# Small matrix products of two recurrent mixers, issued in pairs on the two halves of the TensorE array

## The chip, the cores and the metric

The kernel runs on one core of one Trainium2 chip. The metric is device time in microseconds; the kernel before takes 1673.71 us, the median of 3 runs (1672.53 to 1675.28). The engines of the core work side by side and in program order, each through its own list: TensorE (PE, matrix products; the loads of its stationary operand are listed apart as PEld), VectorE (DVE), ScalarE (ACT), GpSimd (POOL), and SyncE (SP), which here only issues DMA transfers.

## The reference

Two layers, each a mixer and a mixture of experts, over 256 frames of 1024 channels. The mixer sends one projection into three recurrent mixers over chunks of 64 frames: gated DeltaNet (4 heads, state 128x128), retention, and Mamba-2 SSD (2 groups of 8 heads, state 128 by 8x64). The two that matter here:

```python
# gated DeltaNet, per chunk (k, u, w, q of 64 rows; sol = triangular solve)
def step(state, inp):
    q_c, k_c, u_c, w_c, dec_c = inp
    delta = u_c - jnp.einsum('bhlk,bhkv->bhlv', w_c, state)
    state = dec_c[..., None, None] * state + jnp.einsum('bhlk,bhlv->bhkv', k_c, delta)
    return state, jnp.einsum('bhlk,bhkv->bhlv', q_c, state)

# SSD: inside a chunk
y = jnp.einsum('bghcij,bghcjp->bghcip', wmat, xh)
# SSD: from chunk to chunk
def step(state, inp):
    c_c, b_c, x_c, lc_c, dt_c = inp
    y_c = jnp.einsum('bgln,bghnp->bghlp', c_c, state) * jnp.exp(lc_c)[..., None]
    wr = jnp.exp(lc_c[..., -1:] - lc_c) * dt_c
    state = (jnp.exp(lc_c[..., -1])[..., None, None] * state
             + jnp.einsum('bgln,bghlp->bghnp', b_c, x_c * wr[..., None]))
    return state, y_c
```

DeltaNet reads a state that already holds the chunk; SSD reads the state before the chunk. The three outputs are projected, gated, summed and projected again; then a layer norm. The experts are top-2 of 8 in one of 4 groups, 32 experts in all, whose weights are read whole in every layer.

## The kernel before

Frames lie in two tiles of 128 (`tt`), so two chunks of 64 stand in one tile, the even one on partitions 0 to 63 and the odd one on 64 to 127 (`par`, `ps`). A layer has two stages. In the mixer stage, `main` walks 26 blocks of projections (`ORDER`), each cut into pieces of 24 or so matmuls; the weights are split into a high and a low part by ACT (L251) and DVE (L239) and multiplied in three products (`mm3`). Beside it `Weave` steps generators, one step a piece: `delta_chain` (A), `ret_chain` (B), `ssd_chain` (C) and what writes their outputs (`delta_out`, `ret_out`, `ssd_out`). The order on each engine is then set by a scheduler that places every instruction when its simulated operands are ready, so a product of a chain stands between projection products. In the expert stage, 1 MB weight tiles stream in through a ring of buffers (`W`, `ring`), and the buffers come free as PE uses them up.

TensorE multiplies a stationary operand of up to 128 rows by 128 columns. A product with 64 rows lies on the upper or the lower row half (its operands start at partition 0 or 64), one with 64 columns on one column half (its output starts at partition 0 or 64).

The tiles that matter. In `delta_chain`, per chunk c: `pks` = k of the chunk times the old state (L728, four heads, 64 columns), `vb` corrected by it on DVE (L732), `pd` and `dl` (the solve applied, L738 and ACT), `pS` (state increment) and `st` (the new state, DVE), `po` = q times the new state (L761, four heads, 64 columns). In `ssd_chain`, per tile tt and group g: `xdt`, `xw`, `xd` (scaled inputs), `crh`, `crl`, `pcr`, `crm` (decay matrix `dc`), then for both chunks `pi` = c times the old state (64 columns, 512 wide), `pcS` = b times `xw` (64 rows, 512 wide), `cst` the new state (DVE, POOL), `py` = `dc` times `xdt` (eight heads, 64x64); the sum of them is `y`, kept under the name `xdt`. `ssd_out` multiplies y by a gate (POOL, L968), takes squares (ACT) and a root (`crs`), scales (DVE, L981), and `out_T` transposes it (`poT`, L788). `px`, `pn`, `pT` are the 64x64 products of the DeltaNet solve (`bmm`), which walk heads in the outer loop and halves in the inner one.

Of the kernel before, what the change touches and what calls it, by code (L numbers as in the profile page):

```python
# [150 lines left out]
def trunk_kernel(ctx: ExitStack, tc: tile.TileContext, x_in, w_in, w_br, w_g, w_u, w_d, smalls, lnp, consts, out,  # L151
# [95 lines left out]
    def mm(o, l, r, start=True, stop=True):  # L247
        return PE.matmul(o, l, r, start=start, stop=stop)  # L248
# [100 lines left out]
    for l in range(layers):  # L349
# [240 lines left out]
        def delta_chain():  # L590
# [125 lines left out]
            st = None  # L716
# [2 lines left out]
            sso = M(8, "sso")  # L719
            for c in range(4):  # L720
                tt, par = c // 2, c % 2
                ps = slice(64 * par, 64 * par + 64)
                if c:

                    pk = P("pks")
                    for h in range(4):
                        a = (h % 2) * 256 + c * 64
                        mm(pk[ps, h * 128:(h + 1) * 128], kT[h // 2][:, a:a + 64], st[:, h * 128:(h + 1) * 128])  # L728
                    for h in range(4):
                        hs = slice(h * 128, (h + 1) * 128)  # L730
                        n = 4 * tt + h
                        DVE.scalar_tensor_tensor(vb[tt][ps, hs], pk[ps, hs], ckb[ps, n:n + 1], vb[tt][ps, hs],  # L732
                                                 op0=OP.mult, op1=OP.add)
                    yield
                pd = P("pd")
                for h in range(4):
                    hs = slice(h * 128, (h + 1) * 128)
                    mm(pd[ps, hs], Tt[ps, (4 * tt + h) * 64:(4 * tt + h) * 64 + 64], vb[tt][ps, hs])  # L738
                dl = T("dl", True)
                act(dl[ps], pd[ps])  # L740
                yield
                pS = P("pS")
                for h in range(4):
                    hs = slice(h * 128, (h + 1) * 128)
                    mm(pS[:, hs], kend[tt][ps, hs], dl[ps, hs])
                ns = T("st", True)
                if c == 0:
                    DVE.tensor_copy(ns, pS)
                else:
                    for h in range(4):  # L750
                        hs = slice(h * 128, (h + 1) * 128)
                        DVE.scalar_tensor_tensor(ns[:, hs], st[:, hs], ex[:, 2 + par, tt, h:h + 1], pS[:, hs],
                                                 op0=OP.mult, op1=OP.add)
                st = ns
                yield
                if par == 0:
                    po = P("po")
                for h in range(4):
                    hs = slice(h * 128, (h + 1) * 128)
                    a = (h % 2) * 256 + c * 64  # L760
                    mm(po[ps, hs], qT[h // 2][:, a:a + 64], st[:, hs])  # L761
                if par == 1:
                    o = T("ao")
                    DVE.tensor_copy(o, po)
                    junk = T("junk", True)
                    for h in range(4):
                        hs = slice(h * 128, (h + 1) * 128)
                        act(junk[:, hs], o[:, hs], AF.Square, accum_out=sso[:, 4 * tt + h:4 * tt + h + 1])
                    R["ao"].append(o)
# [113 lines left out]
        def ssd_chain():  # L883
# [23 lines left out]
            for tt in range(NT):  # L907
                for g in range(2):
                    hs = slice(4 + 8 * g, 12 + 8 * g)
                    p = P("pxt")  # L910
                    for q in range(4):
                        ch = 4 * g + q
                        PE.transpose(p[:, q * 128:(q + 1) * 128],
                                     xc[ch // 2][:, (ch % 2) * 256 + tt * 128:(ch % 2) * 256 + tt * 128 + 128], ident)
                    xdt, xw, xd = T("xdt"), T("xw", True), T("xd", True)
                    DVE.tensor_mul(o8(xdt), o8(p), bc(spl[:, tt, hs, None], 64))
                    DVE.tensor_mul(o8(xd), o8(p), bc(B["dsk"][:, 8 * g:8 * g + 8, None], 64))
                    POOL.tensor_mul(o8(xw), o8(xdt), bc(ex[:, 1, tt, hs, None], 64))
                    dp = T("crh", True, F32R), T("crl", True, F32R)
                    for d, g_ in zip(dp, R["gcp"]):  # L920
                        POOL.tensor_mul(o8(d), C["e64b"], bc(g_[:, tt, hs, None], 64))
                    yield
                    pr = P("pcr")
                    for d in dp:
                        mm(pr, R["bo_r"], d, d is dp[0], d is dp[1])
                    dc = T("crm", True)
                    yield
                    DVE.tensor_sub(o8(dc), bc(gc[:, tt, hs, None], 64), o8(pr))
                    act(dc, dc, AF.Abs)
                    act(dc, dc, AF.Exp, scale=-1.0)  # L930
                    POOL.tensor_mul(o8(dc), o8(dc),
                                    cb[:, None, (2 * tt + g) * 64:(2 * tt + g) * 64 + 64].to_broadcast([128, 8, 64]))
                    yield
                    yield
                    py, pi = P("py"), P("pi")
                    for par in range(2):
                        c = 2 * tt + par
                        ps = slice(64 * par, 64 * par + 64)
                        if c:
                            a = g * 256 + c * 64  # L940
                            mm(pi[ps], cT[:, a:a + 64], sts[g])
                        if c < 3:
                            pS = P("pcS")
                            mm(pS, btok[ps, (2 * tt + g) * 128:(2 * tt + g) * 128 + 128], xw[ps])
                            ns = T("cst", True)
                            if c == 0:
                                DVE.tensor_copy(ns, pS)
                            else:
                                POOL.tensor_mul(o8(ns), o8(sts[g]), bc(ex[:, 2 + par, tt, hs, None], 64))
                                DVE.tensor_add(ns, ns, pS)  # L950
                            sts[g] = ns
                        for n in range(8):
                            mm(py[ps, n * 64:n * 64 + 64], dc[ps, n * 64:n * 64 + 64], xdt[ps, n * 64:n * 64 + 64])
                        yield
                    y = xdt
                    rows = slice(64, 128) if tt == 0 else slice(0, 128)
                    DVE.tensor_add(y, xd, py)
                    DVE.tensor_mul(o8(xd[rows]), o8(pi[rows]), bc(ex[rows, 0, tt, hs, None], 64))
                    POOL.tensor_add(y[rows], y[rows], xd[rows])
                    R["cy"][tt, g] = y  # L960
                    yield
# [513 lines left out]
```

## Time and profile before

| | |
|---|---|
| runs | 1672.53, 1673.71, 1675.28 us; median 1673.71 |
| profiled execution | 1675.43 us, span 1673.8 us, mean granted clock 0.951 |
| PE busy | 1402.3 us (84%) |
| DVE, ACT, POOL busy | 630.8, 507.9, 180.7 us |
| DMA | 518.93 MB, mean 310 GB/s |
| chain that ended last | PE 51%, DMA 46%, DVE 2% |

The span is what the trace covers from first to last instruction; the execution is 1.6 us longer. Busy is the time in which at least one instruction of an engine ran. Matmuls are pipelined: one that lasts 0.28 us may be followed by the next after 0.12, so starts say more than durations. A float32 product stands in the trace as two matmul records. The chain is followed back from the last instruction, at each step to what released it.

### The profile page before, as it was taken

The page shows a single profiled execution, that of the slowest core. Times are in us where ns is not written, and L with a number is a line of the kernel's source. Part 1 is how long each engine was busy: PE and PEld are TensorE (multiplying, and loading weights), DVE is VectorE, ACT ScalarE, POOL GpSimd, SP SyncE. Part 2 cuts the span into 40 slices and gives each one's busy share as a digit, 9 for nine tenths or more (in the row PEclk, how much of TensorE's full clock was granted, in tenths as well). Part 3 has the DMA queues.
Part 4 walks back from the last instruction along what each step waited for, and adds up shares of the span by engine and source line. Part 5 has one row for each costly group of instructions (what it writes and reads, how often), then busy time and mean ns, then how long its engine had stood idle before and what let it go on. Part 6 is the DMA issues. An engine that isn't in the chain of part 4 may idle for free.

```text
span 1673.8 us, 25789 instructions
## 1 busy us (share of the span) xinstructions
PE 1402.3 (84%) x10568; PEld 891.2 (53%) x10568; DVE 630.8 (38%) x1216; ACT 507.9 (30%) x983; POOL 180.7 (11%) x146
## 2 busy tenths in 40 slices
PE   8999999999967729766699999999998677287775
PEld 8999878995312203221199988789843122022211
DVE  7888667663000000000288876676620000000002
ACT  6856558541000000000067564585310000000000
POOL 0321233200000000000004111332000000000000
PEclk9999999999989869989889999999999999699888
DMA  9544333779999999999974342338799999999996
GB/s 379 193 129 150 102 101 126 282 294 387 421 422 420 420 422 421 421 422 421 393 293 152 127 152 77 126 112 324 285 387 420 421 422 420 421 421 421 422 420 253
DMA packets 90410, 518.93 MB, mean 310 GB/s; under 512 B 10032, under 2 KB 10416, under 8 KB 41904
## 3 DMA queue, kind: packets, MB, share of 16 engines
q1 hardware_dynamic: 90288, 517.24, 77.7%
q8 instruction: 85, 1.39, 0.3%
q14 instruction: 37, 0.30, 0.1%
HBM read 516.15 MB, written 1.05 MB: 309 GB/s over the span
## 4 chain that ended last, share of the span: by engine, by line
PE 51%; DMA 46%; DVE 2%; issue 0%; ACT 0%; SPq 0%; DVEq 0%
DMA w<-in_w_u_dram 16%; DMA w<-in_w_d_dram 15%; DMA w<-in_w_g_dram 14%; PE g L248 8%; PE pbr L248 6%; PE cx L248 3%; PE pout L248 3%; PE cz L248 3%; PE pg L248 2%; PE pdn L248 2%; PE cbc L248 1%; PE pu L248 1%; PE aq L248 1%; PE bq L248 1%; PE az L248 1%; PE av L248 1%
## 5 line engine op out<-in xcount | busy, mean ns | idle before, releaser
L239 DVE TENSOR_TENSOR hi<-w,hi 128x512 fp32r<-128x512 f32 x400 | 322.9, 822 | 106.0 <-ACT hi L251 41.0
L1278 DVE TENSOR_TENSOR hr<-h,pu 128x256 f32<-128x256 f32 x32 | 16.7, 598 | 743.2 <-PE pu L248 743.2
L251 ACT ACTIVATE hi<-w 128x512 fp32r<-128x512 f32 x400 | 244.3, 628 | 168.9 <-PE pbr L248 43.9
L248 PE MATMUL pg<-w,xg 128*32 128x512 f32 x1024 | 184.6, 646 | 112.9 <-DMA w<-in_w_g_dram 112.7
L248 PE MATMUL pu<-w,xg 128*32 128x512 f32 x1024 | 196.6, 688 | 73.4 <-DMA w<-in_w_u_dram 73.4
L248 PE MATMUL pdn<-w,ht 128*32 128x512 f32 x1024 | 146.6, 603 | 29.9 <-DMA w<-in_w_d_dram 17.4
L248 PEld LDWEIGHTS pg<-w,xg 128*32 128x32 f32 x1024 | 39.9, 117 | 244.8 <-issue 142.6
L248 PEld LDWEIGHTS pu<-w,xg 128*32 128x32 f32 x1024 | 44.1, 122 | 212.9 <-DMA w<-in_w_u_dram 131.2
L248 PE MATMUL g<-xh,hi 128*128 128x256 f32 x768 | 143.0, 285 | 0.0
L248 PEld LDWEIGHTS g<-xh,hi 128*128 128x128 f32 x768 | 120.6, 191 | 2.5 <-issue 2.2
L248 PE MATMUL g<-xl,hi 128*128 128x256 f32 x384 | 110.1, 287 | 0.0
L251 ACT ACTIVATE h<-pg 128x512 f32<-128x512 f32 x16 | 9.6, 597 | 320.3 <-PE pg L248 320.3
L248 PEld LDWEIGHTS pdn<-w,ht 128*32 128x32 f32 x1024 | 35.6, 110 | 126.8 <-issue 67.8
L248 PE MATMUL pbr<-yh,hi 128*128 128x256 f32 x512 | 95.2, 285 | 0.0
L251 ACT ACTIVATE xg<-pxg 128x512 f32<-128x512 f32 (+1 forms) x18 | 10.3, 573 | 276.3 <-PE pxg L248 276.3
L1233 POOL TENSOR_TENSOR oh<-oh,cmb 128x256 f32<-128x256 f32 x16 | 10.0, 622 | 775.4 <-DVE oh L1232 708.2
L251 ACT ACTIVATE os<-pdn 128x512 f32<-128x512 f32 x32 | 19.1, 597 | 228.6 <-PE pdn L248 228.6
L248 PEld LDWEIGHTS pbr<-yh,hi 128*128 128x128 f32 x512 | 80.6, 192 | 2.4 <-issue 2.3
L248 PE MATMUL pxg<-oh,x 128*64 128x128 f32 x1024 | 59.9, 274 | 22.4 <-DVE oh L1232 18.8
L248 PEld LDWEIGHTS pxg<-oh,x 128*64 128x64 f32 x1024 | 56.0, 138 | 35.0 <-issue 26.2
L248 PEld LDWEIGHTS g<-xl,hi 128*128 128x128 f32 x384 | 73.5, 191 | 1.3 <-issue 0.7
L248 PE MATMUL pbr<-yl,hi 128*128 128x256 f32 x256 | 72.8, 285 | 0.0
(333 smaller groups left out, 2258.3 us busy)
## 6 DMA issues: line engine op xcount, KB each, us to landing
w<-in_w_g_dram SPq DMA_DIRECT2D x128, 1024.0 KB, 19.8
w<-in_w_u_dram SPq DMA_DIRECT2D x128, 1024.0 KB, 19.8
w<-in_w_d_dram SPq DMA_DIRECT2D x120, 1024.0 KB, 19.8
w<-in_w_in_dram SPq DMA_DIRECT2D x152, 512.0 KB, 4.6
w<-in_w_br_dram SPq DMA_DIRECT2D x48, 512.0 KB, 4.5
w<-in_w_d_dram SPq DMA_DIRECT2D x32, 256.0 KB, 5.9
ln<-in_lnp_dram SPq DMA_DIRECT2D x8, 512.0 KB, 10.6
mc<-in_consts_dram SPq DMA_DIRECT2D x2, 1187.5 KB, 11.2
```

The source lines that it names most:

```text
L239: return DVE.tensor_sub(l, src, lo(h))
L248: return PE.matmul(o, l, r, start=start, stop=stop)
L251: return ACT.activation(o, i, f, **k)
L1233: POOL.tensor_mul(ohv[:, 1], ohv[:, 0], bc(cv[:, :, e:e + EQ, None], PL))
L1278: DVE.tensor_mul(hr.rearrange("p (j k h q) -> p h k q j", j=2, k=2, h=2)[:, hh], v(h), v(pu))
```

## The change

In `delta_chain` the product of k of the next chunk with the state (`pks`) is issued together with q of this chunk with the same state (`po`), head by head in turn; `po` of an even chunk lies on the lower-numbered column half and `pks` of the odd one on the other, and so on. In `ssd_chain` the loop over the two chunks of a tile is taken apart into three steps: first the state products of both (`pcS`, on the two row halves) and the states, then the eight heads of `py` with the two halves in turn, then the read-outs `pi` of both (on the two column halves), from states kept in `before`. A step of the chain more lies in each block (six yields after the decay matrix instead of five).

```diff
             for c in range(4):
                 tt, par = c // 2, c % 2
-                ps = slice(64 * par, 64 * par + 64)
+                ps, ns_ = slice(64 * par, 64 * par + 64), slice(64 - 64 * par, 128 - 64 * par)
                 if c:
 
-                    pk = P("pks")
-                    for h in range(4):
-                        a = (h % 2) * 256 + c * 64
-                        mm(pk[ps, h * 128:(h + 1) * 128], kT[h // 2][:, a:a + 64], st[:, h * 128:(h + 1) * 128])
                     for h in range(4):
...
                 if par == 0:
                     po = P("po")
+                if c < 3:
+                    pk = P("pks")
+
                 for h in range(4):
                     hs = slice(h * 128, (h + 1) * 128)
                     a = (h % 2) * 256 + c * 64
                     mm(po[ps, hs], qT[h // 2][:, a:a + 64], st[:, hs])
+                    if c < 3:
+                        mm(pk[ns_, hs], kT[h // 2][:, a + 64:a + 128], st[:, hs])
...
-                    py, pi = P("py"), P("pi")
-                    for par in range(2):
-                        c = 2 * tt + par
-                        ps = slice(64 * par, 64 * par + 64)
+
+                    cs = [2 * tt + par for par in range(2)]
+                    half = [slice(64 * par, 64 * par + 64) for par in range(2)]
+                    pS = {}
+                    for c in cs:
+                        if c < 3:
+                            pS[c] = P("pcS")
+                    for c, ps in zip(cs, half):
+                        if c < 3:
+                            mm(pS[c], btok[ps, (2 * tt + g) * 128:(2 * tt + g) * 128 + 128], xw[ps])
+                    before = {}
+                    for c in cs:
+                        before[c] = sts[g]
+                        if c < 3:
+                            ns = T("cst", True)
+                            if c == 0:
+                                DVE.tensor_copy(ns, pS[c])
+                            else:
+                                POOL.tensor_mul(o8(ns), o8(sts[g]), bc(ex[:, 2 + c % 2, tt, hs, None], 64))
+                                DVE.tensor_add(ns, ns, pS[c])
+                            sts[g] = ns
+                    yield
+                    py = P("py")
+                    for n in range(8):
+                        ns_ = slice(n * 64, n * 64 + 64)
+                        for ps in half:
+                            mm(py[ps, ns_], dc[ps, ns_], xdt[ps, ns_])
+                    yield
+                    pi = P("pi")
+                    for c, ps in zip(cs, half):
                         if c:
                             a = g * 256 + c * 64
-                            mm(pi[ps], cT[:, a:a + 64], sts[g])
-                        if c < 3:
-                            pS = P("pcS")
-                            mm(pS, btok[ps, (2 * tt + g) * 128:(2 * tt + g) * 128 + 128], xw[ps])
-                            ns = T("cst", True)
-                            if c == 0:
-                                DVE.tensor_copy(ns, pS)
-                            else:
-                                POOL.tensor_mul(o8(ns), o8(sts[g]), bc(ex[:, 2 + par, tt, hs, None], 64))
-                                DVE.tensor_add(ns, ns, pS)
-                            sts[g] = ns
-                        for n in range(8):
-                            mm(py[ps, n * 64:n * 64 + 64], dc[ps, n * 64:n * 64 + 64], xdt[ps, n * 64:n * 64 + 64])
-                        yield
+                            mm(pi[ps], cT[:, a:a + 64], before[c])
+                    yield
```

What stands on PE in the first SSD block of layer 0 (tt 0, g 0), before. The g rows are projection products, written as one of three products each; a count behind a row is the number of equal products.

```order
L248 MATMUL g_2324<-xh_97,hi_2245 128x256
L248 MATMUL py_2226<-xdt_2073,crm_2109 64x64 x8
L248 MATMUL pS_2276<-dl_2224,ktok_730 128x128 x4
L248 MATMUL pi_2227<-cst_2230,cv_1997 64x512
L248 MATMUL pcS_2284<-xw_2074,btok_2014 128x512
L248 MATMUL py_2226<-xdt_2073,crm_2109 64x64 x8
L248 MATMUL g_2324<-xl_98,hi_2245 128x256
```

The same place now, on PE: first the two state products, and further down the products of y.

```order
L248 MATMUL pd_2219<-vb_1134,Tt_1122 64x128 x4
L248 MATMUL pcS_2226<-xw_2074,btok_2014 128x512
L248 MATMUL pcS_2227<-xw_2074,btok_2014 128x512
L248 MATMUL g_2322<-xh_97,hi_2237 128x256
L248 MATMUL g_2322<-xh_97,hi_2240 128x256
...
L248 MATMUL g_2432<-xh_97,hi_2315 128x256
L248 MATMUL pS_2271<-dl_2224,ktok_730 128x128 x4
L248 MATMUL py_2278<-xdt_2073,crm_2109 64x64 x16
L789 MATMUL poT_2299<-cst,bo_1541 128x128 x4
L248 MATMUL g_2432<-xh_97,hi_2314 128x256
```

The second state product moved up beside the first, pi left this place, and the sixteen products of y, eight of each half before, stand in one row, in which the halves take turns.

On PE in the A chain, before: the outputs of chunk 0 (po) and the products of k of chunk 1 with the same state (pks), then the g products that follow.

```order
L248 MATMUL g_2447<-xh_97,hi_2321 128x256
L248 MATMUL po_2349<-st_2281,cv_300 64x128 x2
L248 MATMUL po_2349<-st_2281,cv_385 64x128 x2
L248 MATMUL pks_2354<-st_2281,cv_475 64x128 x2
L248 MATMUL pks_2354<-st_2281,cv_553 64x128 x2
L248 MATMUL g_2447<-xh_97,hi_2320 128x256
```

The same products now, on PE.

```order
L248 MATMUL g_2432<-xh_97,hi_2314 128x256
L248 MATMUL po_2347<-st_2276,cv_300 64x128
L248 MATMUL pks_2348<-st_2276,cv_475 64x128
L248 MATMUL po_2347<-st_2276,cv_300 64x128
L248 MATMUL pks_2348<-st_2276,cv_475 64x128
L248 MATMUL po_2347<-st_2276,cv_385 64x128
L248 MATMUL pks_2348<-st_2276,cv_553 64x128
L248 MATMUL po_2347<-st_2276,cv_385 64x128
L248 MATMUL pks_2348<-st_2276,cv_553 64x128
L248 MATMUL g_2432<-xl_98,hi_2314 128x256
```

The four po and the four pks of a set alternate now; in all three sets of a layer it reads so.

On PE at the end of the SSD chain of layer 0, before: the last py and pi (tt 1, g 1), and further on the first transposes of y (poT).

```order
L248 MATMUL g_3292<-xh_97,hi_3212 128x256
L248 MATMUL py_3194<-xdt_3054,crm_3106 64x64 x8
L248 MATMUL pi_3195<-cst_3199,cv_1997 64x512
L248 MATMUL py_3194<-xdt_3054,crm_3106 64x64 x8
L248 MATMUL g_3292<-xl_98,hi_3212 128x256
...
L248 MATMUL g_3471<-xl_98,hi_3377 128x256
L788 MATMUL poT_3362<-cst,xdt_2073 128x128 x4
L788 MATMUL poT_3410<-cst,xdt_2808 128x128 x4
L248 MATMUL g_3471<-xh_97,hi_3378 128x256
L248 MATMUL g_3471<-xh_97,hi_3377 128x256
```

The same end now, on PE.

```order
L248 MATMUL g_3385<-xh_97,hi_3289 128x256
L248 MATMUL py_3246<-xdt_3155,crm_3189 64x64 x16
L248 MATMUL pi_3263<-cst_2690,cv_1997 64x512
L248 MATMUL pi_3263<-cst_3243,cv_1997 64x512
L248 MATMUL g_3385<-xh_97,hi_3288 128x256
...
L248 MATMUL g_3572<-xl_98,hi_3463 128x256
L789 MATMUL poT_3362<-cst,xdt_2073 128x128 x4
L789 MATMUL poT_3410<-cst,xdt_2886 128x128 x4
L789 MATMUL poT_3500<-cst,xdt_2472 128x128 x4
L789 MATMUL poT_3549<-cst,xdt_3155 128x128 x4
L248 MATMUL g_3572<-xh_97,hi_3464 128x256
```

The last py and pi moved behind 59 more projection products of block g0; all four transposes follow one another in g1, 86 projection products behind pi, where there were 97 behind the last py. On SP the transfers stand in the same order as before.

## Rows read from the trace of the kernel before

**Rows 1.** The page's slices: busy tenths of PE and of DMA, 40 slices

```profile
PE   8999999999967729766699999999998677287775
...
DMA  9544333779999999999974342338799999999996
```

**Rows 2.** The chain of waits in order of time: start us, us, what

```profile
251.26 1.82 PE py L248 x32
...
423.30 19.66 DMA w<-in_w_u_dram
...
828.30 10.18 DMA w<-in_w_in_dram
...
1254.83 19.97 DMA w<-in_w_u_dram
```

**Rows 3.** Stretches of the timeline: stretch, length, busy us of each engine, clock, DMA share

```profile
200.00:300.00 100.00, 99.05 (x652) 80.63 (x651) 65.98 (x113) 67.40 (x131) 31.36 (x23) 1.00 0.35 117
360.00:380.00 20.00, 19.75 (x100) 16.54 (x99) 14.70 (x28) 4.84 (x11) 0.00 (x0) 1.00 0.72 258
```

**Rows 4.** Groups of PE by shape, 0 to 345 us: busy us, mean ns, idle before

```profile
L248 PE MATMUL py<-xdt,crm 64*64 64x64 f32 x128 | 9.0, 222 | 0.0
L248 PE MATMUL pcS<-xw,btok 64*128 64x512 f32 x12 | 6.6, 633 | 0.0
L248 PE MATMUL pi<-cst,cv 128*64 128x512 f32 x12 | 6.4, 618 | 0.9 <-DVE cst L950 0.9
```

**Rows 5.** Timeline of PE, first SSD block: start us, us, what, records

```profile
169.65 0.40 PE L248 MATMUL g<-xh,hi 128*128 128x256 f32 x2
169.89 0.28 PE L248 MATMUL g<-xl,hi 128*128 128x256 f32 x1
170.10 1.08 PE L248 MATMUL pd<-vb,Tt 64*64 64x128 f32 x8
171.11 1.12 PE L248 MATMUL pcS<-xw,btok 64*128 64x512 f32 x2
172.17 0.50 PE L248 MATMUL g<-xh,hi 128*128 128x256 f32 x2
```

**Rows 6.** Timeline of PE, a product group of the DeltaNet solve

```profile
91.39 1.15 PE L248 MATMUL px<-Tn,bt 64*64 64x64 f32 x32
92.47 0.39 PE L248 MATMUL cx<-xl,hi 128*128 128x256 f32 x1
```

**Rows 7.** Timeline of PE, end of the SSD chain

```profile
270.12 1.14 PE L248 MATMUL py<-xdt,crm 64*64 64x64 f32 x16
271.20 1.07 PE L248 MATMUL pi<-cst,cv 128*64 128x512 f32 x2
272.20 1.14 PE L248 MATMUL py<-xdt,crm 64*64 64x64 f32 x16
...
285.19 1.09 PE L788 MATMUL poT<-cst,xdt 128*128 128x128 f32 x8
```

**Rows 8.** Timeline of PE, first set of po and pks

```profile
181.96 0.76 PE L248 MATMUL po<-st,cv 128*64 128x128 f32 x5
182.45 0.32 PE L248 MATMUL pks<-st,cv 128*64 128x128 f32 x1
182.56 0.27 PE L248 MATMUL po<-st,cv 128*64 128x128 f32 x1
...
182.83 0.71 PE L248 MATMUL pks<-st,cv 128*64 128x128 f32 x5
183.47 0.39 PE L248 MATMUL g<-xh,hi 128*128 128x256 f32 x1
```

**Rows 9.** The page's groups: a product of the expert stage

```profile
L248 PE MATMUL pg<-w,xg 128*32 128x512 f32 x1024 | 184.6, 646 | 112.9 <-DMA w<-in_w_g_dram 112.7
```

**Rows 10.** Timelines of POOL and DVE behind the last pi

```profile
277.46 1.63 POOL L968 TENSOR_TENSOR xdt<-xdt,z 128x512 f32<-128x512 f32 x1
...
284.65 1.67 DVE L981 TENSOR_SCALAR xdt<-xdt,crs 128x512 f32<-128x512 f32 x4 [0.83 <-ACT crs L251]
```

## The prediction

> **What bounds the kernel now.** I read the page's slices first: TensorE (PE) is busy in 9 tenths or more in slices 2 to 9 and 21 to 28, and the DMA engines are near full in between and at the end [rows 1]. So each layer has a mixer stage and an expert stage. The chain of waits says who sets the end [rows 2]: it runs through PE matmuls up to 423.30 us, from there through expert weights up to 828.30, through PE again up to 1254.83, and through expert weights to the end. The reader is to see that the products of the change lie inside the PE parts (in layer 0 between about 171 and 273 us, and the chain walks through py itself at 251.26). In 200 to 300 us PE is busy for 99.05 of 100 us at granted clock 1.00 while DMA moves at a share of 0.35; at 360 to 380 us, where the expert weights have begun, DMA is at 0.72 [rows 3]. Its queue is then held by full buffers and not by bandwidth, so what PE finishes earlier also frees the buffers earlier, and the expert stage starts earlier by the same amount. I take one microsecond saved on PE in a mixer stage as one microsecond of the end.
>
> A busy PE is not PE at its peak, so the price of a product is the step from one start to the next, not its duration. A 128x256 projection product starts every 0.12 us (two records between 169.65 and 169.89), and the step into another tiling of the array is 0.21 (169.89 to 170.10) [rows 5]: a change of tiling costs 0.09 us. Each float32 product is two records in the trace.
>
> **The change part by part, one layer.** All numbers are start to start.
>
> The y products (py): 64 products, 128 records, 9.0 us of busy time, 70 ns a record [rows 4]. Before, eight products of one half stand in a row: 16 records take 1.08 us (270.12 to 271.20) [rows 7]. The solve of the DeltaNet chain already has this 64x64 form with the halves in turn: 32 records of px take the same 1.08 us (91.39 to 92.47), 34 ns each [rows 6]. So a pair runs in the time of one, and each of the four blocks of a layer goes from 2.16 to 1.08 us. That is 4.3 us; I take 4.0, because one of the four already runs both halves back to back and has no tiling change to lose.
>
> The Trainium skill speaks against this (TensorEngine Tiling (Array Packing), Restrictions and Gotchas): different row tiles cannot use one PSUM bank at the same time. Both halves of py write one bank, so by that rule the 4.0 us of each layer would be missing and the time would be 8 us higher. The px row contradicts it: its halves write one bank too, on different partitions, and run in half the time; the row decides.
>
> The state products (pcS, 64 rows by 512 columns): 1.06 us each (171.11 to 172.17) [rows 5]. Two pairs a layer stand side by side now, those of chunks 0 and 1; chunk 2 stays alone. No row of before shows two products on the two row halves with all 128 output columns. Bounds: no overlap and one tiling change more, a loss of 0.1 us a pair; full overlap, a gain of 1.0. The nearest rows are px, whose halves differ in rows and columns, and pg, 32-column products of 512, four to the array, at 184.6/1024 = 0.18 us a record [rows 9] against pi's 6.4/12 = 0.53 [rows 4]. Both overlap nearly in full, so I take 1.0 a pair, 2.0 a layer.
>
> The read-outs (pi, 64 columns by 512): 1.00 us each (271.20 to 272.20) [rows 7]. The pairs of chunks 2 and 3 stand side by side, two a layer, on two column halves of one bank, as pg does. I take 0.95 each, 1.9; at worst nothing.
>
> The DeltaNet outputs and the next chunk's products (po, pks): in three sets a layer, eight products (16 records) that were four and four. The first took 1.51 us (181.96 to 183.47) [rows 8]. From the fifth po at 182.45 to 182.83 seven records start, 55 ns each, po and pks in turn, where the last po and the first pks overlapped anyway. At that step 16 records take 0.88, with 0.15 for entry and exit 1.03: 0.5 saved a set, 1.5 a layer. The other two sets had other work between their products and could give a little more.
>
> Tiling changes: over this stretch the order of PE goes from 61 to 47. My spans above hold the way out but not the way in, so I count half of the 14, 7 x 0.09 = 0.6 us.
>
> The second pi waited 0.9 us for the state cst [rows 4]. Its pair now stands about 40 projection products behind the last state product. This wait goes: 0.9.
>
> Sum of one layer: 4.0 + 2.0 + 1.9 + 1.5 + 0.6 + 0.9 = 10.9 us.
>
> What it adds: the last py and pi of the SSD chain come later, and the transposes of its y (poT) behind them. Before, the last pi ends at about 272.20 and poT starts at 285.19 [rows 7]; between them lie two DVE steps, two on POOL (the last from 277.46), a square and a root on ACT, and the scaling on DVE at 284.65 [rows 10]. In the new order 86 projection products, 86 x 0.12 = 10.3 us, stand between pi and poT, against 97 (11.6 us) behind the last py. If the chain kept its 284.65 - 272.20 = 12.5 us and 0.4 for the first scaling, PE would stand 2.6 us a layer; if POOL and ACT take it up at once, as their idle time there allows, it fits. Queued behind the waiting poT is all of g1 and the A branch, so this wait would count in full. I put 0.9 a layer. No other consumer moves nearer to its producer than some 2 us of projection products, and the DMA queue issues the same transfers in the same order, none of them moved past another.
>
> Two layers: 2 x (10.9 - 0.9) = 20.0 us. The profiled execution took 1675.43 us (span 1673.8 and 1.6 around it); it becomes 1655.4. The median of the runs, 1673.71, lies 1.7 lower: 1653.7 us.
>
> **Rivals.** *The 512-column pairs overlap by half or not at all.* If the second record of the first product must start before the first record of the second product, only the middle of each pair runs together. Eight such pairs in two layers lose 0.5 each: 1657.7; with no overlap 1.0 each: 1661.7. Against it: pks starts at 182.45, ahead of a po at 182.56 that stands before it in the order [rows 8]. For it: no row shows a full pair of 512. The Trainium skill has such a rule (TensorE: Matmul & The Clock Gate, Packing small matmuls): matmuls start strictly in program order. By that rule, the first of these two times; the po and pks rows disagree with it.
>
> *The tail stalls PE.* The chain from pi to poT keeps its 12.9 us and PE stands 2.6 us a layer, or up to 5 if the ACT queue, which holds splits for the next projections behind the square, falls behind too: 2 x 1.7 to 2 x 4.1 on top, 1657 to 1662.
>
> *Nothing arrives at the end.* If a transfer on the way to the expert stage had no slack, the weights would land when they land now: 1674, or 1664 if only one layer loses it. Against it DMA's 0.35 and 0.72 [rows 3].
>
> *Slower.* The same tail, but longer: PE keeps order, so a y that reaches poT later than 10.3 + 10.9 = 21 us after pi eats the whole gain of the layer, and everything above is loss. At 23 us, about what the chain needs if each of its steps on ACT and DVE first waits for a 0.6 us split and each POOL step doubles, it is 2 x 2 = 4 us slower: 1678. The chain of before took 13.
>
> That the products do not stand in pairs at all is excluded by the order: they do.
>
> **Chances.** My forecast (1649 to 1657) 0.72; half or no overlap 0.13; a stalling tail 0.08; nothing or one layer only 0.04; slower 0.03. The low end: no wait in the tail (1.8) and the other two po sets giving 1 us more in each layer: 1650, with 2 to spare 1648. The high end takes in the pairs without overlap, 1663. 0.2% (3.3 us) is about what a measurement of this kernel can tell from no change. Faster 0.94, same 0.03, slower 0.03.
>
> **What would show it.** In the profile after: py near 35 ns a record instead of 70; the two pcS of a pair starting within 0.1 us of each other and the next product about 1.05 us later, likewise pi; 16 records of po and pks in about 1.0 us; no wait of pi for cst; the chain leaving PE for expert weights near 413 us and again near 1235. Wrong would be: pcS or pi at 2 us a pair; PE idle before poT for more than a microsecond; a chain that enters DMA at 423 as now.

## The result, and the profile after

The changed kernel takes 1650.87 us, the median of 4 runs (1650.05 to 1654.18); beside it the kernel before took 1674.42 (4 runs, 1672.53 to 1675.28). The ratio is 0.9865 with a 95% interval of [0.9848, 0.9882]. The forecast was 1653.7 (1648 to 1663). The profiled execution of the kernel after took 1651.17 us, its span 1649.5, 24.3 shorter than before.

The page's slices, after, answer to [rows 1]:

```profile
PE   8999999999867628767699999999998676387665
...
DMA  9534233879999999999974343338799999999996
```

Both mixer stages are still the stretches in which PE is at 9 tenths, and behind them DMA becomes full again at once. The chain of waits, after (start us, us, what), shows where the time that is saved goes:

```profile
257.80 7.78 PE g L248 x65
265.57 1.08 PE py L248 x32
266.65 1.01 PE pi L248 x4
267.66 10.50 PE g L248 x86
278.16 0.01 issue
278.18 1.94 PE poT L789 x16
...
389.83 10.63 DMA w<-in_w_g_dram
...
1209.96 9.22 DMA w<-in_w_g_dram
```

The reader is to see three things. The two rows py and pi hold 32 and 4 records now, and each lasts as long as one half did in [rows 7]. The tail behind them is 86 g products, as the order said, and "issue", time for which the profile names no releaser, is 0.01 us. And the chain enters expert weights at 389.83 us and 1209.96, where before it was 423.30 and 1254.83 [rows 2]: DMA's share at 360 to 380 us rose from the 0.72 of [rows 3] to 0.92:

```profile
200.00:300.00 100.00, 99.99 (x727) 85.78 (x726) 77.16 (x121) 68.17 (x132) 38.23 (x27) 1.00 0.38 130
360.00:380.00 20.00, 18.36 (x109) 13.10 (x110) 15.28 (x60) 2.91 (x9) 0.67 (x1) 1.00 0.92 362
```

(Columns as in [rows 3]. The stretches begin some 13 us further on in the program than the same ones of before, so the second row is to be read for its DMA share alone.)

The groups of PE by shape, 0 to 336 us, after, answer to [rows 4]:

```profile
L248 PE MATMUL py<-xdt,crm 64*64 64x64 f32 x128 | 5.0, 222 | 0.0
L248 PE MATMUL pcS<-xw,btok 64*128 64x512 f32 x12 | 4.5, 641 | 0.0
L248 PE MATMUL pi<-cst,cv 128*64 128x512 f32 x12 | 4.3, 618 | 0.0
```

The mean of one record is unchanged (222 against 222 ns, 641 against 633, 618 and 618). Only the busy time, the union over records, fell: they lie on top of one another. The 0.9 us that pi waited for cst is gone from the last column. The first pair of pcS, on PE's timeline (start us, us, what, records):

```profile
169.22 0.70 PE L248 MATMUL pd<-vb,Tt 64*64 64x128 f32 x5
169.85 1.13 PE L248 MATMUL pcS<-xw,btok 64*128 64x512 f32 x4
170.91 0.50 PE L248 MATMUL g<-xh,hi 128*128 128x256 f32 x2
```

Four records, two whole products, take 1.06 us (169.85 to 170.91), exactly what two records took in [rows 5]. Two products on the two row halves, each with all 128 columns, run fully side by side; this is the case of which no row of before told. The first set of po and pks:

```profile
176.59 0.32 PE L248 MATMUL po<-st,cv 128*64 128x128 f32 x1
176.60 0.32 PE L248 MATMUL pks<-st,cv 128*64 128x128 f32 x1
...
177.41 0.27 PE L248 MATMUL pks<-st,cv 128*64 128x128 f32 x1
177.61 0.38 PE L248 MATMUL g<-xl,hi 128*128 128x256 f32 x1
```

The two of a pair start 0.01 us apart, and 16 records take 1.02 us, where they took 1.51 [rows 8].

To set the terms of the forecast beside the trace I summed, for each name, the steps from the start of a record to the start of the next one on PE, from the first product of the mixer stage (aq) to the first of its output (pout). Layer 0, us:

| | forecast gain | before | after | gain |
|---|---|---|---|---|
| py | 4.0 | 8.35 | 4.67 | 3.68 |
| pcS | 2.0 | 6.21 | 4.22 | 1.99 |
| pi | 1.9 | 6.02 | 4.02 | 2.00 |
| po, pks | 1.5 | 6.22 | 4.24 | 1.98 |
| all else: pi's wait 0.9, tiling changes 0.6, less 0.9 for the tail | 0.6 | 315.39 | 313.50 | 1.89 |
| mixer stage | 10.0 | 342.19 | 330.65 | 11.54 |

In layer 1 the four named rows are the same to 0.01 us, and the stage goes from 345.48 to 333.63, a gain of 11.85. What follows each mixer stage, to the next one's start or the end, stays: 486.15 and 487.00 us before, 486.50 and 487.03 after. The span's 24.3 us are thus 11.54 + 11.85 = 23.4 from the two mixer stages, 1.3 from an earlier first product (11.7 us against 13.0; it lay between 11.2 and 13.6 in the runs below, whatever the kernel), less 0.4.

Part of layer 1 is the granted clock. At the start of that stage it still stands at 0.50, the lower of its two levels (1.2 of 2.4 GHz): for all of the first 4.0 us in the kernel before, and for some 3.3 us in the kernel after (0.59 on the mean of 4 us). In another execution of the same kernel, the control below, it was 1.00 from the start, and the stage took 332.54 us instead of 333.63. With all of py issued twice (below) it was 0.50 again. The four stretches in this order (before, after, control, py twice), columns as in [rows 3]:

```profile
841.20:845.20 4.00, 4.00 (x18) 3.77 (x18) 4.00 (x7) 3.37 (x7) 0.66 (x1) 0.50 1.02 404
828.80:832.80 4.00, 4.00 (x21) 3.78 (x21) 4.00 (x8) 3.32 (x7) 0.75 (x1) 0.59 1.02 407
829.20:833.20 4.00, 3.78 (x31) 3.57 (x31) 4.00 (x7) 3.65 (x8) 0.45 (x1) 1.00 1.01 401
831.00:835.00 4.00, 4.00 (x19) 3.77 (x19) 3.96 (x7) 3.25 (x7) 0.82 (x1) 0.50 1.01 403
```

So a difference of 1 to 1.5 us between two stages of layer 1 need not come from an edit. In layer 0 the clock is 1.00 throughout the stage in all of the runs.

### The profile page after: what moved, and what is told of

Read it like the earlier page. It is cut to its first block, busy times and chain, and to the rows that moved or that the text cites. A ratio compares the mean times of both kernels' runs of the same rounds, so it can differ in the third digit from the quotient of the medians.

```text
span 1649.5 us, 25789 instructions
## 1 busy us (share of the span) xinstructions
PE 1381.2 (84%) x10568; PEld 878.9 (53%) x10568; DVE 640.5 (39%) x1216; ACT 503.4 (31%) x979; POOL 183.5 (11%) x146
## 4 chain that ended last, share of the span: by engine, by line
DMA 51%; PE 47%; DVE 1%; ACT 0%; issue 0%; SPq 0%; DVEq 0%
DMA w<-in_w_d_dram 19%; DMA w<-in_w_u_dram 17%; DMA w<-in_w_g_dram 13%; PE g L248 9%; PE pbr L248 6%; PE cx L248 3%; PE cz L248 3%; PE pout L248 3%; PE cbc L248 1%; PE aq L248 1%; PE bq L248 1%; PE az L248 1%; PE av L248 1%; PE ak L248 1%; PE bk L248 1%; PE bg L248 1%
## 5 line engine op out<-in xcount | busy, mean ns | idle before, releaser
L239 DVE TENSOR_TENSOR hi<-w,hi 128x512 fp32r<-128x512 f32 x400 | 330.9, 846 | 86.1 <-ACT hi L251 40.1
## 6 DMA issues: line engine op xcount, KB each, us to landing
mc<-in_consts_dram SPq DMA_DIRECT2D x2, 1187.5 KB, 11.4
```

The lines of the kernel that those rows point to most:

```text
L239: return DVE.tensor_sub(l, src, lo(h))
```

## The experiments

The theory: on PE a pair takes the time of one product, the mixer stage shrinks by that, and the rest of the layer moves up unchanged, so the end comes earlier by the sum. The rivals: the gain comes from the new order (fewer tiling changes, a wait less) and not from the overlap; or one part is worth nothing. Ratios are to the kernel before on the same chip, 5 rounds each; "the stage" means the sums from aq to pout of layers 0 and 1, in the profiled execution, as above.

**Both parts by themselves.** First the DeltaNet part alone: `ssd_chain` as before, the edit in `delta_chain` kept (see the diff of the change, lines with `pks`).

> Only the DeltaNet half of the change (po and pks issued together); the SSD chain stays as before. Theory (products on free halves run at the same time, and PE time saved in the mixer stage arrives at the end): po and pks together fall by up to 2.0 us a layer, from 6.2 to 4.2 us start to start; the order of PE alternates them only in part here, so 2 to 4 us in both layers, 1670 to 1672 us. Rival (the gain is the regrouping: fewer changes of tiling, and the vanished wait of pi for cst): 61 changes of tiling stay 61 and the wait stays, so no change, 1674.

Measured: 1674.5 us beside 1674.69, ratio 0.9996 [0.9987, 1.0005]: no gain, so this expectation failed. The stage is 341.89 and 345.29 us, and po with pks fell only from 6.22 to 5.95: the first set took 1.29 us instead of 1.51, the other two, with other products still between theirs, 1.53 and 1.96 instead of 1.58 and 1.97. Then the SSD part alone: `delta_chain` as before.

> Only the SSD half of the change; the DeltaNet chain stays as before. Theory: the rest of the gain, about 20 us, 1654 to 1655; po and pks at 5.0 to 6.2 us start to start, since their last and first products overlap anyway. Rival (regrouping): the tiling changes fall to 47 as in the full change, so the full gain, 1651.

Measured: 1652.65 us, ratio 0.9866 [0.9851, 0.9881], the whole gain as far as a run can tell; the interval, 1649.7 to 1654.8 us, holds 1651 as well as most of 1654 to 1655, so the median doesn't tell the two sides apart. The stage is 331.77 and 333.34. Though `delta_chain` is written as before, the sum of po and pks fell to 5.04, 1.2 of the 2.0 us. Its first set stands four and four and takes 1.51 us as before. In the second nothing else stands between the products any more, and the scheduler put them nearly in turn (1.07 us instead of 1.58); in the third they take turns in part (1.29 instead of 1.97). That leaves 0.8 us a layer for the DeltaNet part. The first set of this kernel and the start of the second, PE's timeline:

```profile
178.68 0.76 PE L248 MATMUL po<-st,cv 128*64 128x128 f32 x5
179.18 0.32 PE L248 MATMUL pks<-st,cv 128*64 128x128 f32 x1
179.28 0.27 PE L248 MATMUL po<-st,cv 128*64 128x128 f32 x1
...
179.39 0.27 PE L248 MATMUL po<-st,cv 128*64 128x128 f32 x1
...
179.56 0.71 PE L248 MATMUL pks<-st,cv 128*64 128x128 f32 x5
...
195.06 0.32 PE L248 MATMUL po<-st,cv 128*64 128x128 f32 x1
195.06 0.32 PE L248 MATMUL pks<-st,cv 128*64 128x128 f32 x1
```

On PE's list all four po of the first set stand ahead of the four pks. A product is two records, so the five po records in front are two products and the first record of the third, and the row at 179.28 is the third's second record. The first pks starts at 179.18, ahead of the fourth po at 179.39, as in [rows 8]. About half of such a set overlaps without being written in turn, and writing it in turn gives 0.5 us there and less in the other two.

**Was it only the order that failed in the first of these?** There the scheduler had put other products in between, and po and pks did not take turns throughout. Held in the written order:

```diff
-                    mm(po[ps, hs], qT[h // 2][:, a:a + 64], st[:, hs])
+                    tc.keep_in_program_order(mm(po[ps, hs], qT[h // 2][:, a:a + 64], st[:, hs]))
...
-                        mm(pk[ns_, hs], kT[h // 2][:, a + 64:a + 128], st[:, hs])
+                        tc.keep_in_program_order(mm(pk[ns_, hs], kT[h // 2][:, a + 64:a + 128], st[:, hs]))
```

> e1 again (the DeltaNet part of the change alone, SSD as before), with po and pks held in the written order, so that all three sets of a layer take turns. Theory (e1 gained nothing because its po and pks do not take turns: 6.2 to 5.95 us a layer only): po and pks fall to 4.4 to 5 us a layer, 1.2 to 1.8 us less in each, 1671 to 1672.5 beside 1674.5 of before. Rival (the DeltaNet part brings nothing even where its products take turns, since PE then waits elsewhere): 1674 to 1675.

Measured: 1680.9 us (1677.48 to 1684.87) beside 1674.87, ratio 1.0044 [1.003, 1.0058]: slower, which neither side expected. po with pks did fall, to 5.00 (1.2 less a layer), but the stage grew to 343.29 and 348.12. PE's waits in layer 0, 12 to 346 us (engine, line, waited for: us in total, times, longest):

```profile
PE pi L248 <- DVE cst L951: 2.3, 2, 1.4
PE py L248 <- POOL crm L932: 0.7, 1, 0.7
PE poT L789 <- DVE xdt L982: 0.5, 1, 0.5
```

Of these only 0.9 at pi stood there before [rows 4]. PE now meets products of the old, unpaired SSD chain before their operands are there. The 1.4 more at pi, 0.7 at py and 0.5 at poT are 2.6 us, twice what the pairs saved. Layer 1 has the same waits but grew by 2.64 us where layer 0 grew by 1.10, and in it the granted clock fell to 0.50 in the middle of the stage:

```profile
1102.00:1109.00 7.00, 6.88 (x33) 5.15 (x34) 3.85 (x6) 2.98 (x8) 1.52 (x3) 0.51 0.46 154
```

Just before, PE had stood 0.67 us before a py and 0.90 before a pi; 16 records of py then took 1.90 us, where [rows 7] has 1.07. In layer 0 PE stood as long at these two and the clock stayed at 1.00. The profiled execution was the fastest of the six, 1677.48 us, 2.05 above that of before. Where the others lose 1 to 7 us more isn't settled; more falls of the clock are possible, but no trace of those runs shows it.

**py: pairs or order?** The changed kernel, with the two loops of py exchanged, so that eight products of one half are followed by eight of the other:

```diff
-                    for n in range(8):
-                        ns_ = slice(n * 64, n * 64 + 64)
-                        for ps in half:
+                    for ps in half:
+                        for n in range(8):
+                            ns_ = slice(n * 64, n * 64 + 64)
```

> The changed kernel, but the eight heads of py are issued first all on one half and then all on the other, in one row of sixteen as in the change; the rest is untouched, tiling changes 45. Theory: py goes back from 36 to about 66 ns a record start to start, 3.7 us a layer, 7 to 8 us in all: 1658 to 1659. Rival (regrouping): py stands in the same blocks, so 1651. A third reading, that the array queues are deep enough to overlap eight products of one half with eight of the other: also 1651.

Measured: 1656.54 us, ratio 0.9888 [0.9873, 0.9903]; py 7.27 us a layer, all other named sums within 0.2 of after, the stage 332.87 and 337.10. Its last block on PE's timeline:

```profile
268.39 1.90 PE L248 MATMUL py<-xdt,crm 64*64 64x64 f32 x32
270.21 1.08 PE L248 MATMUL pi<-cst,cv 128*64 128x512 f32 x4
```

32 records in 1.82 us are 57 ns each, against 34 in turn (1.08 us) and 68 for one half alone [rows 7]. So of py's 3.68 us a layer, 2.6 come from the turns (7.27 less 4.67) and 1.08 from bringing both halves to one place. Most of that 1.08 is overlap too. Two separate blocks take 2.16 us, two adjoining ones 1.82 (one block of the kernel before already did, at 251.26 [rows 2]): in the trace the second half starts beside the thirteenth of the first half's sixteen records, so its first two products run beside the other's last two. With po and pks it was the same, the fifth of eight records. The theory and the rival both hold a part, the theory the larger; the expectation was some 2 us too high.

**The 512-column pairs apart.** The changed kernel, with a step of the chain between the two pcS of a pair and between the two pi:

```diff
+                            if c == 0:
+                                yield
...
+                    py, pi = P("py"), P("pi")
+                    if tt:
+                        mm(pi[half[0]], cT[:, g * 256 + 128:g * 256 + 192], before[2])
+                        yield
...
-                        if c:
+                        if c % 2:
```

> The changed kernel, but the two pcS of a pair and the two pi of a pair stand apart in the order of PE (other products between them), py and po/pks still in pairs; tiling changes 56 instead of 47. Theory: four pairs a layer lose about 1.0 us each, and 9 changes of tiling cost 0.09 each: 2 x 4.8 = 9.6 us, 1660 to 1661; more if the later SSD tail now makes PE wait. Rival (regrouping alone): only the tiling changes, 1.6 us, 1652 to 1653.

Measured: 1664.18 us, ratio 0.9936 [0.9922, 0.995], 3 us above the expectation. pcS is back at 5.79 and pi at 6.02; the rest is smaller: pd rose by 0.8 and py fell by 0.35, since a block of py no longer stands among products of pd; PE waits 0.6 us for operands (pcr 0.4, poT 0.2); and the projections rose by 1.8. The nine more tiling changes are 0.8 us at the forecast's price, so they explain a part of this; where the rest of it comes from isn't shown. The stage is 336.72 and 339.67, 6 us longer than after. The groups, 0 to 340 us:

```profile
L248 PE MATMUL pcS<-xw,btok 64*128 64x512 f32 x12 | 6.6, 633 | 0.0
L248 PE MATMUL pi<-cst,cv 128*64 128x512 f32 x12 | 6.4, 618 | 0.0
```

These are the busy times of [rows 4] again, without the wait. Undoing the four pairs costs 3.6 us of the 6; the rest comes with the places in which the products stand.

**Does one microsecond on PE count in full?** The changed kernel with all of py issued twice, the second time over the first:

```diff
-                    for n in range(8):
-                        ns_ = slice(n * 64, n * 64 + 64)
-                        for ps in half:
-                            mm(py[ps, ns_], dc[ps, ns_], xdt[ps, ns_])
+                    for _ in range(2):
+                        for n in range(8):
+                            ns_ = slice(n * 64, n * 64 + 64)
+                            for ps in half:
+                                mm(py[ps, ns_], dc[ps, ns_], xdt[ps, ns_])
```

> The changed kernel with every block of py computed twice (the second time over the first; the result is the same). It adds 4 blocks of 1.08 us of paired products in each layer and nothing else on PE. Theory (in the mixer stage the end follows PE one for one): 8.2 to 8.6 us longer, 1659 to 1660. Rival (part of PE's time there is hidden, so that the end follows it by less): 4 us or less longer, 1655 or below. If SSD's y comes too late for its transposes, PE also stands before poT, which the profile would show.

Measured: 1656.97 us, ratio 0.9894 [0.9878, 0.9911], and the unchanged kernel after beside it:

> The changed kernel once more, as a control on the chip of these runs: 1651 us, 23 to 24 us below the kernel before. Every theory expects the same.

Measured: 1652.03 us, ratio 0.9866 [0.9849, 0.9882]. py rose to 8.41 us a layer, 3.74 more (I had put 4.3; a double block pays its entry and its way out once), 7.5 in all. The stage is 333.61 and 337.27 us against 330.64 and 332.54 in the control. Layer 0 grew by 2.97: py's 3.74, less 0.8 by which steps of the projections (g, az) became shorter. Layer 1 grew by 4.73, but 1.5 of it lies at its start, where the granted clock was 0.50 here and 1.00 in the control (rows above). The profiled executions differ by 6.9 (1657.05 and 1650.18), the medians by 4.9. The expectation was 2 to 3 us too high, 1.1 of it by py itself. So most of what PE spends arrives; that each microsecond arrives at the median of the runs is shown no better than to a third.

**The same pairing where the change left it out.** pd (64 rows, 64 columns) still runs all four heads on one half. Changed kernel, with odd heads written to the other column half, and ACT's copy of them in two:

```diff
-                    mm(pd[ps, hs], Tt[ps, (4 * tt + h) * 64:(4 * tt + h) * 64 + 64], vb[tt][ps, hs])
+                    mm(pd[ps if h % 2 == 0 else ns_, hs], Tt[ps, (4 * tt + h) * 64:(4 * tt + h) * 64 + 64], vb[tt][ps, hs])
...
-                act(dl[ps], pd[ps])
+                v2 = lambda t: t.rearrange("p (a b d) -> p a b d", a=2, b=2)
+                for b, qs in ((0, ps), (1, ns_)):
+                    act(v2(dl[ps])[:, :, b], v2(pd[qs])[:, :, b])
```

> The changed kernel, and the same idea carried on to pd, the one product of 64 columns left that stands alone: two of its four heads go to the other column half of the array (their results to the other partitions, from where ACT copies them back in a second, shorter copy). Theory: pd's eight records a chunk go from 109 to 55 ns each, 0.44 us a chunk, 3.5 us in two layers: 1647 to 1648. Rival (the two halves share their 64 rows of input, and the stationary loads of the same rows do not overlap): no change, 1651, or a little slower for eight more ACT copies.

Measured: 1651.53 us, ratio 0.9858 [0.9842, 0.9875]: pd fell from 3.83 to 2.25 us a layer, 1.58 where 1.76 was expected, so its two halves do overlap and the rival's reason is out. But the stage is 330.34 and 333.09, only 0.3 and 0.5 us shorter than after, and the end did not move (the control beside it took 1652.03); a miss. PE's waits in 12 to 346 us:

```profile
PE poT L791 <- DVE xdt L998: 0.9, 1, 0.9
```

The tail that the forecast feared is here. It is told by ACT's timeline, first of the kernel after:

```profile
272.61 0.63 ACT L251 ACTIVATE junk<-xdt 128x512 f32<-128x512 f32 x1 [0.29 <-POOL xdt L983]
273.15 0.18 ACT L251 ACTIVATION_READ_ACCUMULATOR junk<-xdt 128x1 f32 x1
273.24 0.62 ACT L251 ACTIVATE hi<-w 128x512 fp32r<-128x512 f32 x1
273.88 1.28 ACT L251 ACT_TABLE_LOAD   x1
275.17 0.30 ACT L251 ACTIVATE crs<-ssc,mc 128x4 f32<-128x4 f32 x1
```

and the same place with pd on both halves:

```profile
273.95 0.19 ACT L251 ACTIVATION_READ_ACCUMULATOR junk<-xdt 128x1 f32 x1
274.04 0.82 ACT L251 ACTIVATE gt<-g,sb 128x256 f32<-128x256 f32 x2
274.75 0.63 ACT L251 ACTIVATE hi<-w 128x512 fp32r<-128x512 f32 x1
275.40 1.28 ACT L251 ACT_TABLE_LOAD   x1
276.70 0.30 ACT L251 ACTIVATE crs<-ssc,mc 128x4 f32<-128x4 f32 x1
```

Counted from the stage's first product, the square comes 1.15 us earlier here (259.77 us behind it instead of 260.92). With work shifted by so little, two gate steps (gt) come to stand between the square (junk) and the root (crs), 2.75 us instead of 2.02, and PE, with the same 86 products to run behind pi, waits. Two experiments take the wait away by issuing the first transposes later, once with pd on both halves and once without:

```diff
-        def out_T(y, scale, keep, of=(None, None)):
+        def out_T(y, scale, keep, of=(None, None), late=False):
...
-                for h in range(4):
-                    PE.transpose(p[:, h * 128:(h + 1) * 128], y[tt][:, h * 128:(h + 1) * 128], ident)
+                with tc.issue_after(newest["mm"].ins) if late else ExitStack():
+                    for h in range(4):
+                        PE.transpose(p[:, h * 128:(h + 1) * 128], y[tt][:, h * 128:(h + 1) * 128], ident)
...
-                yield
-                R["yC"] += yield from out_T(yy, B["ncw"][:, 4 * g:4 * g + 4], True, (None if g else "mb", None))
+                for _ in range(1 if g else 6):
+                    yield
+                R["yC"] += yield from out_T(yy, B["ncw"][:, 4 * g:4 * g + 4], True, (None if g else "mb", None), g == 0)
```

(`newest["mm"]` is the last product of the projection piece issued so far.)

> The kernel after, with pd on the two halves in turn (as in e6) and the transposes of the first SSD outputs (poT) issued later, 103 projection products behind the last pi instead of 86. Theory (a saving on PE arrives at the end unless an engine then waits; in e6 the 1.6 us of pd per layer were eaten by PE waiting 0.9 us at poT for DVE and by 0.3 to 0.5 us more elsewhere): the wait at poT goes, pd's saving arrives, about 3 us below the kernel after, 1647.5 to 1648.5. Rival (the tail had nothing to do with it; pd's saving is lost in the main products or at a start of a stage): about 1651, as e6.

Measured: 1648.49 us (1647.71 to 1648.83), ratio 0.9843 [0.983, 0.9856].

> The kernel after with the later transposes alone (102 projection products behind the last pi instead of 86). Theory: PE waited at poT for only about 0.2 us a layer in the kernel after, so at most 0.4 us: 1650.5 to 1652, no difference that can be measured. Rival (the tail of the kernel after costs more than the gap before poT shows, as the 0.9 us a layer of the forecast): about 2 us less, 1649.

Measured: 1650.36 us (1650.26 to 1653.14), ratio 0.9855 [0.9841, 0.9869]. PE's timeline of the first of the two, where poT begins:

```profile
279.46 0.28 PE L249 MATMUL g<-xh,hi 128*128 128x256 f32 x1
279.58 0.60 PE L793 MATMUL poT<-cst,xdt 128*128 128x128 f32 x4
```

poT starts 0.12 us behind the last g, the step without a wait; in the kernel after it is 0.30, poT at 278.18 and a g at 277.88. The stage is 328.82 and 331.95, 1.83 and 1.68 shorter than after: about pd's 1.58 and the 0.2 of the gap, though other products moved by up to 0.3 us both ways. So the wait at poT, 0.9 of the 1.58 us a layer, was the larger part of what ate pd's gain, and with later transposes the kernel is the fastest of all here: its runs lie some 2 us below those of the kernel with later transposes alone, on the same chip, with no overlap of the ranges, though the intervals of the two ratios still touch. Later transposes without pd gain nothing that can be told, as the theory said.

## Why the prediction was right

**The bound** was right. In 200 to 300 us PE is busy for 99.99 of 100, and the expert stages kept their lengths within 0.4 us, so what PE saved came off the end. One sub-forecast, the chain leaving PE near 413 and 1235 us, failed: it left at 389.83 and 1209.96. Before, PE rows still carried the chain behind pout up to 423.30; after, expert weights carry it from 389.83 on. That changes who is named last, not the length of the stage.

**py** (4.0 forecast, 3.68 measured): right, and of it 2.6 by turns, 1.1 by place. The rule weighed there, from the Trainium skill (TensorEngine Tiling (Array Packing), Restrictions and Gotchas), is not what this trace shows: 32 records on both halves, writing one bank on different partitions, take 1.08 us, as 16 on one half did.

**pcS and pi** (2.0 and 1.9; measured 1.99 and 2.00): right. The rival of half or no overlap is out: 1.06 us for four records of pcS, 1.01 for four of pi. The row of pg supported this less than I took it to: 0.18 us a record against 0.53 is 2.9 products at a time, not four. The order of starts that the Trainium skill gives (TensorE: Matmul & The Clock Gate, Packing small matmuls), applied to single records, would have made a pair 1.5 us by the forecast's estimate; the traces disagree with it for whole products too, with the first pks at 179.18 ahead of the fourth po at 179.39. The rows that the forecast set against it, 182.45 and 182.56, don't bear on it: the po at 182.56 is the second record of a product that had already started.

**po and pks** (1.5 forecast, 1.98 measured): the price of a set in turn was right (1.03 forecast, 1.02 measured), and the first set gave the 0.5. The other two gave 0.56 and 0.95, since other products had stood between theirs. The DeltaNet edit isn't needed for all of it: 1.2 came with the SSD part alone, after which two of the sets stood in turn or nearly, and 0.8 is what the written turns add; alone, the DeltaNet edit has no measurable effect.

**The wait of pi** (0.9): gone, as said. Tiling changes and the small rest were put at 0.6 and measure 1.0 (1.89 less 0.9).

**The tail** is the term that was mis-sized: 0.9 us a layer was held back, and nothing was lost. PE's step into poT is 0.30 us before and after, 0.18 more than between two g. I had kept the chain's old length, 12.5 us from the end of the last pi. But a py stood behind that pi, and y needs it too: 1.07 us of the 12.5 were PE's own work [rows 7]. And in the new place the chain is shorter: from the end of the last py or pi to the first scaling on DVE it takes 9.95 us (267.59 to 277.54) and took 11.4 (273.27 to 284.65 [rows 10]). Before, DVE put a split of weights between its two steps on y, and ACT still had a table load of 1.28 us and two gate steps ahead of the square:

```profile
273.38 0.69 DVE L957 TENSOR_TENSOR xdt<-xd,py 128x512 f32<-128x512 f32 x1 [0.18 <-PE py L248]
274.11 0.69 DVE L239 TENSOR_TENSOR hi<-w,hi 128x512 fp32r<-128x512 f32 x1
274.72 0.68 DVE L958 TENSOR_TENSOR xd<-pi,ex 128x512 f32<-128x512 f32 x1
...
277.70 1.28 ACT L251 ACT_TABLE_LOAD   x1
278.99 0.84 ACT L251 ACTIVATE gt<-g,sb 128x256 f32<-128x256 f32 x2
279.72 0.63 ACT L251 ACTIVATE junk<-xdt 128x512 f32<-128x512 f32 x1
```

(DVE and ACT of the kernel before.) Now the two DVE steps follow one another (267.65 and 268.43) and ACT's are done when y arrives. The split costs about 0.5 of the 1.4 us, ACT 0.6, and a longer step on POOL 0.2. This margin is an accident of the order: the experiment with pd shows the wait, 0.9 us a layer, after a shift of a microsecond. With it, the two stages gain 23.4 us where the sum said 20.0: 1.8 for the tail, 1.0 for po and pks, and 0.6 for the other terms together. The median came out 2.8 us below the forecast.

The slower rival didn't happen in this kernel, but its mechanism, PE standing before what a chain hasn't finished, is real: holding po and pks in order with the old SSD chain made the kernel 0.4% slower, with 2.6 us of such waits a layer, most of them at pi and py.

## What to carry to other kernels

In these runs two products on different row or column halves took the time of one when they stood next to each other on PE's list. In blocks the last two products of one half overlapped with the first two of the other: about half of the gain in blocks of four, a third in blocks of eight. Price the pair from start-to-start steps, and what the move does to the rest (tiling changes, waits gone) separately: here that was 1.9 of a layer's 11.5 us. Ask also how much of the overlap the order would give without being written: 1.1 us of py's and 1.2 of po's and pks's came from bringing the products together. A saving on the bounding engine arrives only as long as no consumer comes early enough to wait, so look at the chain behind the moved products, and give it more independent work before the next use if it is within a microsecond, as it was here with pd.

## What was not expected of the hardware

Products on the two row halves with all 128 output columns overlap as fully as quarter-array ones (four records in 1.06 us), and the two of a pair start 0.01 us apart. Overlap of blocks had a reach of two products: the other half starts beside the fifth of eight po records and beside the thirteenth of sixteen py records, so 64x64 products in blocks of eight still cost 57 ns a record against 34. And on ACT each of the two root steps of the tail is preceded by a table load of 1.28 us, 2.56 of the tail's 9.95.
